# A longer modelled way from a transfer's end to its use, and two rings at the arena's other end

## The chip, the cores and the metric

The kernel runs on one core of a Trainium2 chip. The metric is the device time of one execution in microseconds (us). Engines are named as in the profile: PE is TensorE (PEld its weight loads), DVE is VectorE, ACT is ScalarE, POOL is GpSimd, SP is SyncE. POOL and SP compute next to nothing here: their queues issue the transfers.

## The reference, cut to what matters

A two-layer encoder trunk on 272 tokens of width 2048, in float32. Each layer is a mixer (an attention half and a state-space half, side by side) and a channel mixer (dense in layer 0, the best 2 of 8 experts in layer 1).

```python
for layer in range(2):
    hn = rms_norm(h, mix_norm[layer])
    c_q, c_kv, k_rope, u = jnp.split(hn @ w_in[layer], splits, axis=-1)
    att = mla_attention(c_q, c_kv, k_rope, ...)          # 8 heads
    ssm = s5_mixer(u, ...)                               # 64 groups of 16 channels, state 64, both directions
    mixed = jnp.concatenate([rms_norm(att, ...), rms_norm(ssm, ...)], -1)
    h = h + mixed @ w_out[layer]
    hn = rms_norm(h, ffn_norm[layer])
    h = h + (swiglu(hn, ...) if layer == 0 else moe_swiglu(hn, ...))
out = rms_norm(h, final_norm)[:, 16:]
```

`s5_mixer` is a linear recurrence over the tokens. It is computed here in chunks of 4 tokens: an input product per group (X), a scan over 68 chunks, and an output product per group (y).

## The kernel before

All weights (some 550 MB) stream from HBM once in blocks of 512 KB through a class `Stream` (five `raw` buffers; a high and a low part, `wh` and `wl`, are made of each block by ACT and DVE, and three products stand for one of float32). The first 40 blocks, of layer 0's mixer, are used as plain float32 (`raw` itself is the operand); one such product shows as two records in the trace.

**What sets the order.** The program is one stream of instructions, and every engine works its own part of it off strictly in order. Which instruction is written next is decided while the program is built: `Sched.run` holds a main generator (`mixer`, `dense`, `experts`) and a list of side generators. A generator yields a condition or a time; it goes on when the planner's clock, `Model.t["PE"]`, has come to it. `Model` keeps for each 16 bytes (or so) of memory the time at which it was last written and last read; `Model.run` moves an engine's time on by a planned cost, and `Model.dma` plans a transfer: issue 0.5 us (0.6 us on POOL's queue), 0.65 us, then the elements of the target at 90 per ns; `mark("DMA", ...)` then enters the end plus `OUT["DMA"]` as the time from which the target can be used (and the source written over). `Kern.rdy(...)` is that time plus 0.2 us, and a side generator that uses loaded data yields it ahead of its instructions. So `OUT["DMA"]` says how late after a transfer its users are written into the program. The hardware waits with semaphores in any case; only the order is planned.

**The chain around the change, in each mixer.** The main generator computes eight tiles of `u` (`u_tile`, 16 products of 128 x 272 each, in the order 0, 4, 1, 5, 2, 6, 3, 7). Each tile is scaled by DVE and put into the DRAM scratch `uscr` through POOL's queue (`put_u`). When the tiles `qb` and `qb + 4` are there, `ssm_x` loads them back in another layout (`load_u`, two transfers of 136 KB on POOL's queue), and its input products (`128x136` on PE, two for each group, between the products of `u`) read them. In layer 0 the matrices V of these products are made by DVE at that time (`v_make`, two `128x512` products of `ssm_bT` and `pscr` loads), as are the output matrices W and the Toeplitz blocks (`w_all`, `toep`: four products of `64x96` on PE; loads of `ssm_bz` and `ssm_C`). In layer 1 V and W were made ahead during `dense`. Then come the scan on DVE (`ssm_scan`), attention on PE (`attention`), and, once attention is over, the copies of the state (`ssm_h`, ring `rh`) and the output products (`ssm_y`, `68x64` on PE, ring `ry`), between the products of the first half of `w_out`. The gate's products (`w_glu`) behind it need all of `ssm_y`.

**Memory.** `Arena.get` hands out stretches of one large tile, first fit from the low end or, with `top=True`, from the high end; `room` asks whether requests fit, always from the low end.

Of the kernel before, what the change touches and what calls it, by code (L numbers as in the profile page):

```python
# [24 lines left out]
NC = 68  # L25
TC = 4
# [43 lines left out]
class Arena:  # L70


    def __init__(self, t, n):
        self.t, self.n, self.live = t, n, []
        self.peak = 0
# [52 lines left out]


class Ring:  # L130
    def __init__(self, arena, n, shape, p=128):
        self.h = [arena.get(shape, p) for _ in range(n)]
        self.i = 0

    def next(self):
# [109 lines left out]
class Model:  # L245


    OUT = {"PE": 197.0, "DVE": 127.0, "ACT": 152.0, "DMA": 960.0}

    def __init__(self):  # L250
        self.t = {"PE": 0.0, "DVE": 0.0, "ACT": 0.0, "DGE": 0.0, "DMA": 0.0}
# [84 lines left out]
    def mark(self, eng, e, ins, outs):  # L336
        e += self.OUT[eng]
        for ap in ins:
            n, u = self.where(ap)
            if u is not None:  # L340
                r = self.mem[n][1]
                r[u] = np.maximum(r[u], e)
        for ap in outs:
            n, u = self.where(ap)
            if u is not None:
                self.mem[n][0][u] = e

    def dma(self, q, out, *ins):
        t = max(self.q.get(q, 0.0), self.ready(*ins))
        n, u = self.where(out)  # L350
        if u is not None:
            t = max(t, self.mem[n][0][u].max(), self.mem[n][1][u].max())
        t = max(t, self.t["DGE"]) if q != "pool" else t
        e = t + (500.0 if q != "pool" else 600.0)
        self.q[q] = e
        if q != "pool":
            self.t["DGE"] = e
        d = max(self.t["DMA"], e + 650.0) + size_all(out) / 90.0
        self.t["DMA"] = d
        self.mark("DMA", d, ins, [out])  # L360
        if self.log is not None:
            self.log.append(("DMA", d - size_all(out) / 90.0, d, "dma"))
        return d + 960.0


def size_all(ap):
    n = 1
    for x in ap.shape:
        n *= x
    return n  # L370
# [161 lines left out]
class Kern:  # L532
# [568 lines left out]
    def ssm_h(self, l, F):  # L1101

        nc, st = self.nc, self.st
        yield self.has("scan", l)
        yield self.has("att", l)
        yield lambda: F.room(2 * 4 * 2 * NC)
        X = st["X"]
        rh = st["rh"] = Ring(F, 2, [4, 2, NC])
        st["hq"], st["hn"], n = [], 0, 0
        for t in rh.h:  # L1110
            nc.vector.memset(t.ap, 0.0)
        for T in TORD:
            for a in (0, 4):
                yield lambda: n - st["hn"] < 2
                t = rh.next()
                yield self.s.m.clear(t)
                g = 8 * T + a
                nc.scalar.activation(t[0:64, :, :, 1:NC],
                                     X[0:64, :, :, g:g + 4].rearrange("p s r g -> p g r s"), AF.Copy)
                nc.vector.tensor_copy(t[64:128, :, :, 0:NC - 1],  # L1120
                                      X[64:128, ::-1, :, g:g + 4].rearrange("p s r g -> p g r s"))
                st["hq"].append((t, self.rdy(t)))
                n += 1
# [153 lines left out]
    def ssm_y(self, l, F):  # L1277

        nc, st = self.nc, self.st
        q0 = NMETA if l else 0  # L1280
        N, k0 = L - q0, q0 // TC
        yield self.has("scan", l)
        yield lambda: "rh" in st and self.R is not None and F.room(8 * N, 512, 512) and self.R.room(8 * N, 8 * N)
        R = self.R
        g_ = st["g"] = F.get([8, N], top=True)
        gh, gl = st["gh"], st["gl"] = R.get([8, N]), R.get([8, N])
        ry = Ring(F, 2, [TC, 8, 16], NC)
        idn = self.cst[:NC, CI:CI + NC]

        def turn(T, y, t):  # L1290
            yield t
            bank = yield from self.grab()
            ps = bank[:, :L].rearrange("p (t k) -> p t k", t=TC)
            for j in range(TC):
                nc.tensor.transpose(ps[:, j], y[:, j].rearrange("p g c -> p (g c)"), idn)
            nc.scalar.activation(g_[:, T].rearrange("p (k t) -> p t k", t=TC), ps[:, :, k0:], AF.Gelu_apprx_tanh)
            self.drop(bank)
            nc.scalar.activation(gh[:, T], g_[:, T], AF.Copy)
            yield self.rdy(gh[:, T])
            nc.vector.tensor_tensor(gl[:, T], g_[:, T], gh[:, T].bitcast(F32), op=OP.subtract)  # L1300
            st["nT"] += 1

        st["nT"] = 0
        for i, T in enumerate(TORD):
            yield lambda: i in st["wq"]
            w, m, u, t = st["wq"].pop(i)
            yield t
            yield lambda: i - st["nT"] < 2
            y = ry.next()
            bank = yield from self.grab()  # L1310
            ps = bank[:NC].rearrange("p (g t c) -> p g t c", g=8, t=TC)
            for a in (0, 4):
                yield lambda: len(st["hq"]) > 0
                H, t = st["hq"].pop(0)
                yield t
                for g in range(4):
                    b = (a + g) // GW[l], (a + g) % GW[l]
                    for r in range(2):
                        nc.tensor.matmul(ps[:, a + g], H[:, g, r], w[:, b[0], r, :, b[1]], start=(r == 0), stop=False)
                    nc.tensor.matmul(ps[:, a + g], u[:, a + g, T // 4],  # L1320
                                     m[:, a + g].rearrange("p (t c) -> p t c", t=TC), start=False, stop=True)
                    if g % 2:
                        yield None
                st["hn"] += 1
            st["yn"] = i + 1
            nc.scalar.activation(y.rearrange("p t g c -> p g t c"), ps, AF.Copy)
            self.drop(bank)
            self.s.add(turn(T, y, self.rdy(y)))
        yield lambda: st["nT"] == 8
        for r in (ry, st["rh"], st["U"], st["X"]) + st["rw"]:  # L1330
            r.free()
        self.flags.add(("Y", l))
# [1058 lines left out]
```

## Time and profile before

| | us |
|---|---|
| device time, median of 3 runs | 2499.2 (2496.71 to 2500.32) |
| profiled execution | 2494.38 |
| its span, first to last instruction | 2492.5 |
| PE busy | 2427.1 (97%) |
| DVE busy | 1920.4 (77%) |
| ACT busy | 1375.0 (55%) |

In time, layer 0's input products begin at 47 us and layer 1's at 1311.60 us; all compute instructions carry line 408, that of the helper through which they are written, so groups are told apart by their tiles (`fa` is the float32 arena, `bank` a bank of PSUM). Ends of matmuls are modelled, so PE's waits are read from the idle time that stands in brackets ahead of a row, and its speed from the starts of rows that follow each other.

### The profile page before, as it was taken

The numbers are of one execution on the slowest core, as the hardware profiler recorded it, in microseconds if no ns is written. First come the engines' busy times: TensorE is split into PE (matmuls) and PEld (weight loads), VectorE is DVE, ScalarE is ACT, GpSimd is POOL, SyncE is SP. The second block draws the span as 40 slices with busy tenths as digits, with TensorE's granted clock in tenths as the row PEclk, the third lists the DMA queues.
The fourth block names the chain that finished last, engine by engine and source line by source line (L and its number), as shares of the span: only waits on it lengthen the run. The fifth ranks groups of instructions, "written<-read, shape, count | busy, mean of one in ns | idle before, by whom it ended". The sixth has DMA issues, their size and how long they took to land. (4 is left out here: it accounts for less than half of the span.)

```text
span 2492.5 us, 42294 instructions
## 1 busy us (share of the span) xinstructions
PE 2427.1 (97%) x15930; PEld 2187.0 (88%) x15930; DVE 1920.4 (77%) x3282; ACT 1375.0 (55%) x1876; POOL 152.2 (6%) x262
## 2 busy tenths in 40 slices
PE   8899999999999999999999899999999999999997
PEld 6676699999999999999999759987888888888886
DVE  8788657787766666555666987668999999999997
ACT  4324566443333333334455456546777877877775
POOL 3400110011100000000011001000000000000000
PEclk9999899999999999999999989999999999999998
DMA  7842554568755555555566316657999999999995
GB/s 258 230 149 86 141 157 151 167 215 269 261 187 194 188 191 190 172 177 170 178 205 195 127 44 204 236 201 271 387 355 350 385 341 371 365 330 372 360 336 198
DMA packets 192919, 583.47 MB, mean 234 GB/s; under 512 B 36225, under 2 KB 48897, under 8 KB 191553
## 3 DMA queue, kind: packets, MB, share of 16 engines
q1 hardware_dynamic: 174802, 520.42, 60.0%
q0 software_dynamic: 17040, 57.97, 7.7%
q8 instruction: 127, 2.08, 0.3%
q10 hardware_dynamic: 864, 2.28, 0.3%
q14 instruction: 86, 0.70, 0.1%
HBM read 560.14 MB, written 22.54 MB: 234 GB/s over the span
## 5 line engine op out<-in xcount | busy, mean ns | idle before, releaser
L408 DVE TENSOR_TENSOR wl<-raw,wh 128x1024 fp32r<-128x1024 f32 (+1 forms) x559 | 667.6, 1202 | 194.2 <-ACT wh L408 188.4
L408 ACT ACTIVATE wh<-raw 128x1024 fp32r<-128x1024 f32 (+1 forms) x559 | 579.8, 1040 | 318.9 <-PE bank L408 231.4
L408 PE MATMUL bank<-XH,wh 128*128 128x272 f32 (+1 forms) x2160 | 636.8, 295 | 0.8 <-ACT tmpr L408 0.5
L408 PE MATMUL bank<-XH,wl 128*128 128x272 f32 (+1 forms) x2160 | 623.0, 288 | 3.1 <-DVE wl L408 3.1
L408 PE MATMUL bank<-XL,wh 128*128 128x272 f32 (+1 forms) x2160 | 620.8, 287 | 1.6 <-DVE XL L408 1.3
L408 PEld LDWEIGHTS bank<-XH,wh 128*128 128x128 f32 x2160 | 407.6, 189 | 5.1 <-ACT tmpr L408 0.7
L408 PEld LDWEIGHTS bank<-XH,wl 128*128 128x128 f32 x2160 | 407.1, 188 | 4.5 <-DVE wl L408 4.5
L408 PEld LDWEIGHTS bank<-XL,wh 128*128 128x128 f32 x2160 | 407.9, 189 | 2.6 <-DVE XL L408 2.2
L408 PE MATMUL bank<-ra,wh 128*128 128x272 f32 (+1 forms) x1792 | 341.1, 290 | 1.8 <-ACT wh L408 1.8
L408 PEld LDWEIGHTS bank<-ra,wh 128*128 128x128 f32 x1792 | 280.7, 188 | 6.5 <-issue 2.4
L408 PE MATMUL bank<-fa 128*68 128x64 f32 (+11 forms) x1892 | 263.5, 279 | 21.9 <-DMA fa<-uscr 10.2
L408 PEld LDWEIGHTS bank<-fa 128*68 128x68 f32 (+6 forms) x1892 | 196.1, 161 | 83.8 <-issue 50.4
L408 DVE TENSOR_TENSOR fa<-fa 128x128 f32<-128x128 f32 (+9 forms) x687 | 236.2, 353 | 43.0 <-ACT fa L408 16.9
L408 PE MATMUL bank<-ra,wl 128*128 128x272 f32 (+1 forms) x896 | 256.6, 286 | 0.8 <-DVE wl L408 0.8
L408 PE MATMUL bank<-wh,XH 128*128 128x512 f32 (+1 forms) x584 | 222.6, 381 | 0.7 <-ACT fa L408 0.4
L408 ACT ACTIVATE fa<-bank 64x268 f32<-64x268 f32 (+9 forms) x281 | 138.6, 500 | 150.4 <-PE bank L408 133.2
L408 PE MATMUL bank<-wh,XL 128*128 128x512 f32 (+1 forms) x584 | 220.1, 377 | 0.0
L408 PE MATMUL bank<-wl,XH 128*128 128x512 f32 (+1 forms) x584 | 219.0, 375 | 0.0
L408 PE MATMUL bank<-wh,ra 128*128 128x512 f32 x552 | 185.7, 393 | 2.0 <-ACT fa L408 2.0
L408 PE MATMUL bank<-fa,raw 128*128 128x272 f32 x608 | 162.4, 405 | 7.2 <-DMA raw<-w_mix 6.4
L408 PEld LDWEIGHTS bank<-ra,wl 128*128 128x128 f32 x896 | 168.6, 188 | 1.0 <-DVE wl L408 1.0
L408 DVE TENSOR_TENSOR wl<-h,wh 128x1024 fp32r<-128x1024 f32 (+1 forms) x137 | 157.0, 1156 | 9.9 <-ACT wh L408 7.4
(127 smaller groups left out, 3232.6 us busy)
## 6 DMA issues: line engine op xcount, KB each, us to landing
raw<-w_dense SPq DMA_DIRECT2D x264, 512.0 KB, 3.4
raw<-w_mix SPq DMA_DIRECT2D x150, 512.0 KB, 3.4
raw<-w_moe_g SPq DMA_DIRECT2D x106, 512.0 KB, 5.5
h<-w_moe_g SPq DMA_DIRECT2D x80, 512.0 KB, 5.8
raw<-w_moe_d SPq DMA_DIRECT2D x73, 512.0 KB, 6.7
h<-w_moe_d SPq DMA_DIRECT2D x59, 512.0 KB, 6.6
raw<-w_moe_t SPq DMA_DIRECT2D x51, 384.0 KB, 4.0
h<-w_moe_t SPq DMA_DIRECT2D x44, 384.0 KB, 4.1
```

Source lines behind the costliest of these rows:

```text
L408: return f(*a, **k)
```

## The change

The planner's figure for the way from a transfer's end to its use is 2260 ns in place of 960 ns, in both places where it stands (the value that `dma` returns is used by nobody). `Ring` gets a `top` argument, and the rings `rh` and `ry` are taken from the high end of their arena. No instruction is added or removed: each engine has the same instructions, of the same shapes, in another order.

```diff
 class Ring:
-    def __init__(self, arena, n, shape, p=128):
-        self.h = [arena.get(shape, p) for _ in range(n)]
+    def __init__(self, arena, n, shape, p=128, top=False):
+        self.h = [arena.get(shape, p, **({"top": True} if top else {})) for _ in range(n)]
...
-    OUT = {"PE": 197.0, "DVE": 127.0, "ACT": 152.0, "DMA": 960.0}
+    OUT = {"PE": 197.0, "DVE": 127.0, "ACT": 152.0, "DMA": 2260.0}
...
-        return d + 960.0
+        return d + 2260.0
...
-        rh = st["rh"] = Ring(F, 2, [4, 2, NC])
+        rh = st["rh"] = Ring(F, 2, [4, 2, NC], top=True)
...
-        ry = Ring(F, 2, [TC, 8, 16], NC)
+        ry = Ring(F, 2, [TC, 8, 16], NC, top=True)
```

On PE the order differs in the first 1,100 of its rows (layer 0's mixer up to the output products) and again in layer 1's mixer (its input products and its output products); `dense`, layer 1's attention and the experts' first pass keep theirs, word for word. On DVE and ACT single instructions move in the same stretches and in `dense`.

PE, layer 0, the second pair of `u` tiles. Its last product stands one row ahead of the first row here (bank_65); from there to the first input product that reads it (the last row) PE has before:

```order
L408 MATMUL bank_66<-fa,raw_99 128x272 x3
L408 MATMUL bank_71<-fa 128x136 x2
L408 MATMUL bank_66<-fa,raw_99 128x272
L408 MATMUL bank_68<-fa 128x136 x2
L408 MATMUL bank_66<-fa,raw_99 128x272 x4
L408 MATMUL bank_66<-fa,raw_100 128x272 x3
L408 MATMUL bank_69<-fa 64x96 x4
L408 MATMUL bank_66<-fa,raw_100 128x272 x3
L408 MATMUL bank_70<-fa 64x96 x4
L408 MATMUL bank_66<-fa,raw_100 128x272 x2
L408 MATMUL bank_71<-fa 128x136 x2
```

and now, where two products, one pair of input products and one Toeplitz block stand between the tile's last product and the first row here:

```order
L408 MATMUL bank_71<-fa 128x136 x2
L408 MATMUL bank_66<-fa,raw_99 128x272 x5
L408 MATMUL bank_68<-fa 128x136 x2
L408 MATMUL bank_66<-fa,raw_99 128x272
L408 MATMUL bank_69<-fa 128x136 x2
L408 MATMUL bank_66<-fa,raw_100 128x272 x2
L408 MATMUL bank_70<-fa 64x96 x4
L408 MATMUL bank_66<-fa,raw_100 128x272 x6
L408 MATMUL bank_67<-fa,raw_96 128x272 x3
L408 MATMUL bank_71<-fa 64x96 x4
L408 MATMUL bank_67<-fa,raw_96 128x272
L408 MATMUL bank_68<-fa 128x136 x2
```

The input product that reads the pair stood behind 16 products, 2 pairs and 2 Toeplitz blocks; it stands behind 20, 4 and 3.

PE, layer 0, the fourth and last pair. The tile's last product stands just ahead of the first row (in bank_66), the first input product that reads the pair is the last row. Before:

```order
L408 MATMUL bank_71<-fa 64x96 x4
L408 MATMUL bank_67<-fa,raw_97 128x272 x8
L408 MATMUL bank_67<-fa,raw_98 128x272
L408 MATMUL bank_68<-fa 64x96 x4
L408 MATMUL bank_67<-fa,raw_98 128x272 x3
L408 MATMUL bank_69<-fa 64x96 x4
L408 MATMUL bank_67<-fa,raw_98 128x272 x3
L408 MATMUL bank_70<-fa 128x136 x2
```

and now:

```order
L408 MATMUL bank_68<-fa 128x136 x2
L408 MATMUL bank_69<-fa 128x136 x2
L408 MATMUL bank_67<-fa,raw_97 128x272 x3
L408 MATMUL bank_70<-fa 64x96 x4
L408 MATMUL bank_67<-fa,raw_97 128x272 x5
L408 MATMUL bank_67<-fa,raw_98 128x272 x3
L408 MATMUL bank_71<-fa 64x96 x4
L408 MATMUL bank_67<-fa,raw_98 128x272 x3
L408 MATMUL bank_68<-fa 64x96 x4
L408 MATMUL bank_67<-fa,raw_98 128x272 x2
L408 MATMUL bank_65<-fa,raw_99 128x272 x2
L408 MATMUL bank_69<-fa 128x136 x2
```

It stood behind 15 products and 3 Toeplitz blocks; it stands behind 18 products, 2 pairs (of the third pair of tiles, moved back likewise) and 3 blocks.

PE, layer 1, the first pair of `u` tiles (here each product is three rows). Before, the first input product of the layer (the row with `128x136`) stands in the middle of the tile that follows the next one, 63 matmuls behind the pair's last:

```order
L408 MATMUL bank_67<-XH,wh_103 128x272
L408 MATMUL bank_67<-XL,wh_103 128x272
L408 MATMUL bank_67<-XH,wl_106 128x272
L408 MATMUL bank_69<-fa 128x136 x2
L408 MATMUL bank_67<-XH,wh_103 128x272
L408 MATMUL bank_67<-XL,wh_103 128x272
L408 MATMUL bank_67<-XH,wl_106 128x272
L408 MATMUL bank_68<-fa 128x136 x2
```

and now it stands behind that tile's end, 96 matmuls behind the pair's last, and three pairs follow each other at once:

```order
L408 MATMUL bank_67<-XL,wh_101 128x272
L408 MATMUL bank_67<-XH,wl_104 128x272
L408 MATMUL bank_68<-fa 128x136 x2
L408 MATMUL bank_69<-fa 128x136 x2
L408 MATMUL bank_71<-fa 128x136 x2
L408 MATMUL bank_65<-XH,wh_102 128x272
L408 MATMUL bank_65<-XL,wh_102 128x272
L408 MATMUL bank_65<-XH,wl_105 128x272
L408 MATMUL bank_70<-fa 128x136 x2
```

In the same way the first pair of layer 0 goes from 25 products and 1 block to 28 and 2, its third from 19 and 3 blocks to 20, 3 blocks and a pair, and layer 1's second, third and fourth pair from 63 matmuls each to 80, 96 and 80.

## Rows read from the trace of the kernel before

**Rows 1.** The page: busy time of each engine with its share of the span, and the clock granted to PE in 40 equal slices (tenths of full speed).
```profile
PE 2427.1 (97%) x15930; PEld 2187.0 (88%) x15930; DVE 1920.4 (77%) x3282; ACT 1375.0 (55%) x1876; POOL 152.2 (6%) x262
...
PEclk9999899999999999999999989999999999999998
```

**Rows 2.** The waits of PE over the whole span, longest in total first: us in total, times, the longest.
```profile
PE bank L408 <- DMA fa<-uscr: 10.2, 5, 3.0
PE bank L408 <- DVE XL L408: 8.4, 7, 1.9
PE bank L408 <- DMA raw<-w_mix: 6.4, 1, 6.4
...
PE bank L408 <- DMA fa<-xtok,fa: 4.5, 2, 3.0
```

**Rows 3.** PE in order of time around the second pair of layer 0: start, us from there to the end of the last in the row, records; in brackets the idle time ahead and what ended it.
```profile
57.88 3.37 PE L408 MATMUL bank<-fa,raw 128*128 128x272 f32 x14
61.18 0.88 PE L408 MATMUL bank<-fa 128*64 128x96 f32 x8
61.98 1.64 PE L408 MATMUL bank<-fa,raw 128*128 128x272 f32 x6
...
68.44 0.92 PE L408 MATMUL bank<-fa 128*128 128x136 f32 x4 [2.71 <-DMA fa<-uscr]
```

**Rows 4.** POOL's queue at the same place: the second tile's store, then the two loads.
```profile
58.87 0.56 POOL L390 DMA_DIRECT2D uscr<-fa  x1
59.42 0.71 POOL L390 DMA_DIRECT2D fa<-uscr  x1
64.63 0.70 POOL L390 DMA_DIRECT2D fa<-uscr  x1 [4.50 <-DMA uscr<-fa]
```

**Rows 5.** PE and POOL at the other places where PE waited for these loads: the first pair of layer 0, the first and the third of layer 1.
```profile
47.05 1.18 PE L408 MATMUL bank<-fa 128*128 128x136 f32 x8 [1.25 <-DMA fa<-uscr]
...
1304.48 0.55 POOL L390 DMA_DIRECT2D uscr<-fa  x1 [7.49 <-issue]
...
1311.60 1.25 PE L408 MATMUL bank<-fa 128*128 128x136 f32 x4 [2.57 <-DMA fa<-uscr]
...
1345.48 0.70 PE L408 MATMUL bank<-fa 128*128 128x136 f32 x4 [0.58 <-DMA fa<-uscr]
```

**Rows 6.** PE at the fourth pair of layer 0, and behind it.
```profile
125.73 0.70 PE L408 MATMUL bank<-fa 128*128 128x136 f32 x4 [3.04 <-DMA fa<-uscr]
126.27 0.62 PE L408 MATMUL bank<-fa,raw 128*128 128x272 f32 x2
126.72 1.02 PE L408 MATMUL bank<-fa 128*128 128x136 f32 x4
127.54 1.11 PE L408 MATMUL bank<-fa,raw 128*128 128x272 f32 x2
128.44 1.11 PE L408 MATMUL bank<-fa 128*128 128x136 f32 x4
129.35 1.06 PE L408 MATMUL bank<-fa,raw 128*128 128x272 f32 x2
130.25 0.94 PE L408 MATMUL bank<-fa 128*128 128x136 f32 x6
```

**Rows 7.** PE at the third pair of layer 0, which did not wait.
```profile
100.43 0.63 PE L408 MATMUL bank<-fa 128*128 128x136 f32 x4
100.89 0.62 PE L408 MATMUL bank<-fa,raw 128*128 128x272 f32 x2
...
102.28 0.40 PE L408 MATMUL bank<-fa 128*128 128x136 f32 x2
```

**Rows 8.** Stretches of the span: from, to, length; busy us of PE, PEld, DVE, ACT and POOL with their records; then PE's granted clock (1.00 is full), the DMA engines' busy share and GB/s.
```profile
68.78:72.19 3.41, 3.41 (x18) 2.94 (x17) 2.19 (x7) 1.69 (x4) 0.00 (x0) 0.50 0.45 112
...
126.80:130.21 3.41, 3.41 (x13) 3.00 (x12) 1.80 (x6) 3.04 (x6) 0.55 (x1) 0.50 0.64 197
1311.23:1314.64 3.41, 3.04 (x13) 3.08 (x14) 0.61 (x1) 0.80 (x2) 0.00 (x0) 0.50 0.32 130
276.99:290.64 13.65, 13.65 (x48) 8.12 (x47) 6.76 (x27) 5.17 (x15) 3.04 (x5) 0.50 0.54 119
1478.48:1495.55 17.07, 16.13 (x37) 8.45 (x37) 13.24 (x55) 5.29 (x15) 0.49 (x1) 0.50 0.00 1
92.67:96.08 3.41, 3.41 (x12) 2.61 (x11) 2.49 (x11) 0.33 (x1) 1.27 (x2) 0.50 0.81 185
...
800.00:850.00 50.00, 50.00 (x401) 48.94 (x400) 33.26 (x52) 17.84 (x20) 1.61 (x3) 1.00 0.60 196
...
1360.00:1480.00 120.00, 108.65 (x683) 89.28 (x682) 107.71 (x326) 65.41 (x140) 0.00 (x0) 0.98 0.31 101
```

**Rows 9.** The instructions on the tile `uscr` in the first 350 us, 8 stores and 16 loads: time from issue to landing.
```profile
DMA to landing us min/median/max: 2.1/5.0/6.2
```

**Rows 10.** DVE at a V product of layer 0, and PE at the Toeplitz block that reads what DVE makes behind it.
```profile
87.42 1.61 DVE L408 TENSOR_TENSOR fa<-fa 128x512 f32<-128x512 f32 x3 [4.01 <-DMA fa<-ssm_bT]
...
91.59 0.35 PE L408 MATMUL bank<-fa 128*64 128x96 f32 x2 [2.17 <-issue]
```

**Rows 11.** PE in order of time at a wait of attention in layer 0 and at one in layer 1.
```profile
275.58 0.41 PE L408 MATMUL bank<-cst,fa 96*16 96x96 f32 x3 [1.21 <-DVE XL L408]
...
1479.05 3.23 PE L408 MATMUL bank<-fa 128*128 128x272 f32 x5 [1.90 <-DVE XL L408]
```

## The prediction, made before the changed kernel ran

> **What bounds the kernel now.** I read the page first: PE is busy for 97% of the span, no other engine for more than 77% [rows 1]. So the time is PE's work plus the moments in which PE stands still or runs slowly, and a change of order alone can only move those. The reader should see how small they are: the listed waits of PE are a few us each, and the largest group, 10.2 us in five waits, is for the loads of `uscr` [rows 2]. The wait for `w_mix` is the start of the kernel and stays.
>
> Next I read PE's timeline at those waits. In layer 0, PE stands 2.71 us ahead of the second pair's first input product [rows 3]; POOL's queue shows why: the store of the second tile is issued at 58.87, the second load can go only when it has landed, at 64.63, and the product starts at 68.44, 9.6 us after the store's issue [rows 4]. The fourth pair waits 3.04 us [rows 6], the first 1.25 us, layer 1's first pair 2.57 us and its third 0.58 us [rows 5]. The third pair of layer 0, whose loads came in time, runs on without a gap [rows 7].
>
> Then the clock. After the waits of 2.71, 3.04 and 2.57 us the granted clock is 0.50 for 3.41 us, the lower of the two levels, 1.2 GHz [rows 8]. Its price is read from equal work: two pairs of input products and two products of `u` take 126.72 to 130.25 = 3.53 us there [rows 6] and 100.43 to 102.28 = 1.85 us at full clock [rows 7]; so 1.7 us each time. No such stretch follows the 1.25 and 0.58 us waits.
>
> **The change part by part.** *The planner's figure.* It adds no instruction. It plans the users of loaded data 1.3 us later, and those behind a store and a load 2.6 us later. By its rules a load of `uscr` took 0.60 + 0.65 + 0.39 + 0.96 = 2.6 us and takes 3.9 now; the trace has 5.0 in the middle of its stores and loads, 2.1 to 6.2 [rows 9]. So the users were written in too early for this chain, and are so still, by less.
>
> What counts on PE is the work that stands between the tile's last product and the first input product. A product of `u` takes (61.18 - 57.88) / 7 = 0.47 us (two records each), a Toeplitz block 61.98 - 61.18 = 0.80 us [rows 3], a pair of input products 100.89 - 100.43 = 0.46 us [rows 7]. With the counts of the order:
> - second pair: 16 x 0.47 + 2 x 0.46 + 2 x 0.80 = 10.0 us before, 20 x 0.47 + 4 x 0.46 + 3 x 0.80 = 13.6 now. 3.6 more covers the wait of 2.71: gain 2.71.
> - fourth pair: 9.45 before, 18 x 0.47 + 2 x 0.46 + 3 x 0.80 = 11.8 now. 2.3 of 3.04 are covered: gain 2.3, and 0.7 stay.
> - first pair: 25 products and 1 block, 12.6, become 28 and 2, 14.8. It gains its 1.25. The third gets 0.9 more and needs none.
> - layer 1: 401 matmuls in 50 us [rows 8] are 0.125 us each; the first and third pair get 33 more, 4.1 us. Gain 2.57 + 0.58. The second and fourth get 2.1 that they don't need.
>
> The waits give 9.4 us, and the three slow-clock stretches that followed them 3 x 1.7 = 5.1 us, if they go as well. Sum 14.5 us.
>
> *What moves along.* V products and Toeplitz blocks move in layer 0. One place there already costs: DVE stands 4.01 us for a load of `ssm_bT`, and 4 us later PE stands 2.17 us at the Toeplitz block that waits for DVE's queue [rows 10], with a slow-clock stretch behind it [rows 8]. Between that V product and that block the order has the same PE work before and now (5 products and a block), so I count it neither gone nor worse. Other blocks come closer to what they read: the 17th stands 0.2 us of PE work behind the last DVE operation on its W, where 2.3 us stood. What this costs is not shown; it is bounded by nothing below (the order leaves it enough if DVE is not late) and by one more such wait, 2.17 + 1.7 = 3.9 us, above. I take half, 2.0.
>
> The stores that SP's queue issues (`wscr`, `escr`) stand elsewhere among the weight loads. PE waited for a weight block in the mixers only at the start [rows 2], and five blocks are under way; so nothing, at worst one wait like the 0.58 us one. The input products end 3 products (1.4 us) later in layer 0's order and 9 matmuls (1.1 us) later in layer 1's, so the scan starts that much later relative to PE. Attention's products cover it. The output products move back by 12 matmuls in layer 0 and 12 to 15 in layer 1. They lie among `w_out`'s first half: their last transpose leaves 210 matmuls, 26 us, ahead of `w_glu` in layer 0 and 60, 7.5 us, in layer 1. So nothing; without this cover, up to 1.9 us.
>
> *The rings at the other end* cost no instruction. What they may add is a wait of the ring's first writer for the last reader of what lay there; the stores of `w_all`, which holds the high end, have been waited for when it is freed. I take nothing, at most one DVE wait of the longest kind here, 4.01 us [rows 10], which PE would see only through the 26 us above.
>
> The experts start in the same order; their `xtok` waits of 4.5 us [rows 2] stay.
>
> Sum: 14.5 - 2.0 = 12.5 us. On the profiled execution, 2494.4 us (its span is 1.9 us less), that makes 2481.9. The median of the three runs is 4.8 us above that execution, and the forecast is made against it: 2499.2 - 12.5 = 2486.7 us.
>
> **The rivals.**
> *The waits move and do not go (no change).* What PE truly lacks may be DVE, which is busy for 107.71 of 120 us in layer 1's attention [rows 8]. PE then reaches attention up to 9 us earlier and gives it back at DVE's queue. For it: the waits for `XL`, 8.4 us in seven [rows 2], are there already, and their order stays. Against it: three of the five waits are in layer 0, and the brackets name the loads. If layer 1's 3.15 + 1.7 and half of layer 0's 9.7 come back, 4.8 - 2.0 = 2.8 us are left: 2496.
>
> *The old figure was right (no change).* If a transfer of this chain landed within the 2.6 us that the planner gave it before, the moved products would only start later, with nothing saved and, by the cover above, nothing lost: 2499. The fastest row is 2.1 us, but the middle is 5.0 [rows 9], and three of the chains end in a wait whose bracket names the load [rows 3, 5, 6]; so 0.04. The Trainium skill, DMA: Bandwidth & Descriptors, section Anatomy of one DMA — SWDGE (gpsimd) path, speaks for this rival: a fixed 2.0 us for a transfer plus its bytes at 436 GB/s, for 136 KB an estimate of 2.3 us by that page. The trace disagrees with it by its 5.0 us.
>
> *Slower: the clock in attention of layer 0.* A wait of only 1.21 us at 275.58 [rows 11] stood ahead of 13.65 us at the lower clock [rows 8]. Attention there is small plain float32 products, and the Toeplitz blocks between its heads move. Each us more at the lower clock costs 0.5 us of PE time; the gain is used up when 25 us more of it fall to 0.50 than now. If 52 us more of it do (four stretches like that one in place of one would be 41 us more), that is 26 - 12.5 = 13 us: 2513. Against it: only that one stretch is slow now, and the order moves blocks by one head at most.
>
> *Faster than forecast.* The same lottery the other way: the stretches of 13.65 and 17.07 us [rows 8], behind waits of 1.21 and 1.90 us [rows 11], cost up to 6.8 and 8.5 us. Layer 1's attention keeps its order, so I give only the first a chance to go: 2480; both: 2471.
>
> **How the numbers follow.** Forecast, 2482 to 2493: 0.50. Faster than that: 0.14. No change, 2494 to 2504: 0.20 for the waits that move and 0.04 for the old figure, 0.24. Slower: 0.12. Within 0.2% (5.0 us) a measurement of this kernel can't tell a change from none; so faster 0.64, same 0.24, slower 0.12. The range reaches from the better case's 2477 to 2503, and leaves out the far ends of the lottery, some 0.17. The forecast's own range is 2482 to 2493: its upper end is the waits alone without the clock and with 3.9 us of new waits (9.4 - 3.9 = 5.5), its lower end all of 14.5 and the block's 2.17.
>
> **What would show it.** In the profile of the changed kernel PE's waits for `fa<-uscr` should be under 2 us in total instead of 10.2, the only one left that of layer 0's fourth pair, about 0.7 us; the granted clock should be 1.00 in the stretches behind the four pairs; PE's wait at the tenth Toeplitz block should still be there. The forecast is wrong if those waits go and the time does not (then look at DVE's waits and at the clock in attention), or if they stay because the store and load land later than 9 us after the store's issue.

## The result, and the profile after

The changed kernel takes 2476.55 us (median of 6 runs, 2475.24 to 2481.03), the kernel before 2496.45 us in the 6 runs beside it (2493.45 to 2500.32). The ratio is 0.9921 with an interval of [0.9908, 0.9934]: 16.5 to 23 us faster, 19.7 in the middle. The forecast was 12.5 us and 2486.7; the time lies 0.45 us below the lower end of the range, 2477.0. The direction and the place were right, the size was too small.

The profiled execution after takes 2478.65 us, its span is 2476.9 us. The page, busy time of each engine and the clock granted to PE in 40 slices, answers to [rows 1]:

```profile
PE 2417.3 (98%) x15930; PEld 2181.0 (88%) x15930; DVE 1920.8 (78%) x3282; ACT 1375.1 (56%) x1876; POOL 151.5 (6%) x262
...
PEclk9999999999999999999999989999999999999998
```

Read it against the span. PE's idle time went from 2492.5 - 2427.1 = 65.4 us to 2476.9 - 2417.3 = 59.6 us, which is 5.8 us; its busy time fell by 9.8 us with the same 15930 instructions. Most of this pair's 15.6 us are therefore not waits but instructions that no longer run at half clock: by the clock records the granted clock is 0.50 for 64.9 us of the trace before and 41.0 us of the trace after, the stretch at the very end left out, and half of the 23.9 us between is 12, a part of which falls into idle time.

The waits of PE over the whole span (us in total, times, the longest) answer to [rows 2]:

```profile
PE bank L408 <- DVE XL L408: 9.3, 8, 1.9
PE bank L408 <- DMA raw<-w_mix: 6.5, 1, 6.5
PE bank L408 <- ACT fa L408: 6.1, 6, 2.0
PE bank L408 <- issue: 4.8, 6, 2.0
PE bank L408 <- DMA fa<-xtok,fa: 4.4, 2, 3.2
...
PE bank L408 <- DMA fa<-uscr: 1.0, 2, 0.7
```

The loads of `uscr` have gone from 10.2 us in five waits to 1.0 in two. But a group's name is what the profile could attribute; PE in order of time at the four pairs of layer 0 and the first of layer 1 (start, us, records, idle time ahead in brackets) shows what is left:

```profile
48.00 0.63 PE L408 MATMUL bank<-fa 128*128 128x136 f32 x4
...
68.41 0.70 PE L408 MATMUL bank<-fa 128*128 128x136 f32 x4 [1.53 <-issue]
...
99.60 0.79 PE L408 MATMUL bank<-fa 128*128 128x136 f32 x4 [2.05 <-issue]
...
101.20 5.00 PE L408 MATMUL bank<-fa,raw 128*128 128x272 f32 x14
...
118.66 0.70 PE L408 MATMUL bank<-fa 128*128 128x136 f32 x4 [0.27 <-DMA fa<-uscr]
...
1311.93 0.70 PE L408 MATMUL bank<-fa 128*128 128x136 f32 x4 [0.72 <-DMA fa<-uscr]
```

The first pair runs on ([rows 5] had 1.25 ahead of it), the fourth keeps 0.27 of 3.04 [rows 6], layer 1's first 0.72 of 2.57. At the second pair 1.53 of 2.71 us remain, and the profile names nothing for them. POOL's queue there answers to [rows 4]:

```profile
57.40 0.55 POOL L390 DMA_DIRECT2D uscr<-fa  x1 [0.31 <-DVE fa L408]
...
62.89 0.69 POOL L390 DMA_DIRECT2D fa<-uscr  x1 [1.20 <-DMA uscr<-fa]
```

The second load is issued 5.5 us ahead of the product; the tile's own view gives 2.4, 5.3 and 8.7 us from issue to landing (shortest, middle, longest) for these transfers, so that this load landed just then is likely and not shown. The wait of 2.05 us at 99.60 is new. Ahead of it DVE waits for a store of W; DVE in order of time:

```profile
94.01 0.63 DVE L408 TENSOR_TENSOR fa<-Wp,fa 128x192 f32<-128x192 f32 x2 [3.31 <-DMA wscr<-fa]
...
102.76 2.28 DVE L408 TENSOR_TENSOR fa<-fa 128x512 f32<-128x512 f32 x4 [1.74 <-DMA fa<-ssm_bT]
```

What is missing from this queue matters more. DVE's waits in the first 200 us of the kernel before, and of the kernel after, by what ended them (us in total, times, the longest):

```profile
DVE fa L408 <- DMA fa<-ssm_bT: 12.4, 5, 4.0
...
DVE fa L408 <- DMA wscr<-fa: 3.6, 3, 1.9
```

```profile
DVE fa L408 <- DMA wscr<-fa: 4.4, 2, 3.3
DVE fa L408 <- DMA fa<-ssm_bT: 2.9, 2, 1.7
```

DVE waited 12.4 us for the loads of `ssm_bT`, from which the matrices V are made, and waits 2.9 now: the longer figure moves the V products away from their loads too. The wait of 4.01 us among them, and the Toeplitz block that stood behind it [rows 10], are gone.

Stretches of the span after (from, to, length; busy us of PE, PEld, DVE, ACT, POOL with records; granted clock, DMA share, GB/s): behind the second pair, behind the wait at 99.60, and attention of layer 0, where [rows 8] has 13.65 us at 0.50.

```profile
68.41:71.82 3.41, 3.41 (x23) 3.04 (x23) 3.31 (x9) 2.60 (x5) 2.62 (x6) 1.00 1.00 316
101.07:104.48 3.41, 3.41 (x11) 2.60 (x10) 1.58 (x3) 1.86 (x3) 0.63 (x2) 0.50 1.01 292
262.00:290.00 28.00, 26.25 (x167) 18.53 (x166) 21.10 (x70) 17.70 (x41) 7.57 (x13) 1.00 0.49 141
```

### The profile page after: what moved, and what is told of

It reads as the page before. It is cut to its first block, busy times and chain, and to the rows that moved or that the text cites. A ratio compares the mean times of both kernels' runs of the same rounds, so it can differ in the third digit from the quotient of the medians.

```text
span 2476.9 us, 42278 instructions
## 1 busy us (share of the span) xinstructions
PE 2417.3 (98%) x15930; PEld 2181.0 (88%) x15930; DVE 1920.8 (78%) x3282; ACT 1375.1 (56%) x1876; POOL 151.5 (6%) x262
## 5 line engine op out<-in xcount | busy, mean ns | idle before, releaser
L408 PE MATMUL bank<-fa 128*68 128x64 f32 (+10 forms) x1892 | 252.9, 272 | 16.5 <-DVE XL L408 5.0
L408 DVE TENSOR_TENSOR fa<-fa 128x128 f32<-128x128 f32 (+9 forms) x687 | 236.6, 353 | 32.6 <-ACT fa L408 15.6
L408 PEld LDWEIGHTS bank<-fa 128*68 128x68 f32 (+5 forms) x1892 | 188.9, 156 | 75.3 <-issue 42.1
```

The costliest lines, as they stand in the source:

```text
L408: return f(*a, **k)
```

## The experiments

The kernels with one part of the change were built from the changed kernel with the figure back at 960 ns, so that their rings lie at the high end. Ratios are against the kernel before in the same series. Edits are quoted in the shortest form that says them.

### Which part

**The rings alone.**

```diff
-    OUT = {"PE": 197.0, "DVE": 127.0, "ACT": 152.0, "DMA": 2260.0}
+    OUT = {"PE": 197.0, "DVE": 127.0, "ACT": 152.0, "DMA": 960.0}
```

> The two rings alone at the arena's high end, the planner's figure at 960 ns. Every engine then has the order of the kernel before, so only addresses differ. Theory (all of the gain is the order): no change, within 3 us of before, the waits for fa<-uscr 10 us in total as before. Rival (the rings' place removes waits for the last readers of the low end): faster by 5 us or more.

Measured 2494.06 against 2497.24, ratio 0.9991 [0.9973, 1.0009]. The theory held: every engine's order is the same as before, and no change is clear of noise. PE's waits for `fa<-uscr` are 14.8 us, not 10; the old order's own executions below reach as far. The opposite part, the longer figure with the rings at the low end, does not exist as a kernel: with it the planner finds no room for the copies of the state or the output products in layer 0. The rings are what lets the longer figure be planned.

**The longer figure in one layer's mixer.** `late` is 1300 in layer 0's mixer and 0 elsewhere, then the other way round.

```diff
-        self.mark("DMA", d, ins, [out])
+        self.mark("DMA", d + self.late, ins, [out])
```

> The longer figure in layer 0's mixer alone (rings high throughout). Theory (layer 0 makes the whole gain, layer 1's is given back at DVE in its attention): 15 to 19 us faster, as much as the whole change within 2 us. Rival (the sum on record, where layer 1 keeps 4.9 us and layer 0's net is 7.7): about 8 us faster, and 5 us or more short of the whole change.

Measured 2487.33, ratio 0.9960 [0.9945, 0.9975]: 10 us, 6 to 14 by the interval. The theory of 15 to 19 fell; the sum on record, 8, lies inside.

> The longer figure in layer 1's mixer alone. Theory (given back at DVE): 0 to 2 us faster; the two waits for fa<-uscr there, 3.15 us, nearly gone, and new waits for wl and wh of about 3 us some 50 us later. Rival (the sum on record): 4.9 us faster.

Measured 2489.21, ratio 0.9976 [0.9959, 0.9993]: 6 us, 1.7 to 10 by the interval. The theory that layer 1's saving is given back at DVE, which I had formed after the result, allowed it 0 to 2 us. The interval alone just touches that; the trace decides against it: layer 1's input products take 56.9 us there, 61.6 to 65.1 in the old order, and its attention 139.7, within the old order's 138.0 to 140.3.

**Layer 0's input products alone.** The longer figure ends with the last input product of layer 0.

```diff
-        self.flags.add(("X", l))
+        self.flags.add(("X", l)); self.s.m.late = 0.0
```

> The longer figure only until the last input product of layer 0 is written; attention, the output products and all that follows are planned with 960 ns. Theory: the order around the input products makes 9 us, and the Toeplitz blocks that it moves into other places of attention decide the clock there, another 4 to 6 us: 13 to 15 us faster, and no stretch of 13.65 us at the lower clock in attention. Rival (planning the rest with the longer figure makes the second part): 9 to 10 us faster.

Measured 2485.44, ratio 0.9959 [0.9942, 0.9976]: 10 us, as much as the longer figure in the whole of layer 0's mixer. The rival's 9 to 10 us lie in the middle of the interval, 6 to 14.5, the theory's 13 to 15 at its end, and its sign failed: a wait of 1.21 us stayed in attention, and the profiled execution has 27.3 us at half clock behind it.

**The whole again.** The changed kernel as it is.

> The changed kernel once more, beside the runs below. Theory (the gain is the waits for the uscr loads and the clock stretches behind them, 14.5 us, and what lies above is scatter of the clock elsewhere): 13 to 17 us faster. Rival (a further gain that the sum on record lacks): 18 to 22 us faster again.

Measured 2478.87, ratio 0.9924 [0.9907, 0.9942]: 19 us. The middle fits the rival, but the interval, 14.5 to 23 us, reaches into the theory's 13 to 17, and the profiled executions below give 16.7: whether the first result was a favourable draw stays open. The layers' 10 and 6 add up to 16; the rest is within the intervals.

### Which transfers

**`uscr` alone, and all but `uscr`.** The edit of the first; the second has the two figures exchanged.

```diff
-        self.mark("DMA", d, ins, [out])
+        self.mark("DMA", d + (1300.0 if any("uscr" in a.tensor.name for a in (out, *ins)) else 0.0), ins, [out])
```

> The longer figure for the transfers to and from uscr alone, 960 ns for all others. Theory (this chain makes the gain): 12 to 16 us faster, PE's waits for fa<-uscr under 3 us in total. Rival (the loads for V, W and the Toeplitz blocks, planned later too, make a good part): 6 to 10 us faster.

Measured 2483.04, ratio 0.9943 [0.9923, 0.9964]: 14 us, 9 to 19 by the interval; the theory held.

> The longer figure for all transfers but those to and from uscr. Theory (the uscr chain makes the gain): within 3 us of before, and PE still waits 8 us or more for fa<-uscr. Rival (the other loads make a good part): 5 to 9 us faster, DVE's wait of 4 us for ssm_bT gone.

Measured 2500.22, ratio 1.0004 [0.9988, 1.0021]: nothing, as the theory had it. PE's waits over the span, first of the `uscr` kernel, then of the other:

```profile
PE bank L408 <- DVE fa L408: 7.4, 6, 3.6
...
PE bank L408 <- DMA fa<-uscr: 2.6, 2, 1.8
```

```profile
PE bank L408 <- DMA fa<-uscr: 15.1, 6, 6.0
```

So the chain through `uscr` is needed, and without it the rest is worth nothing: what DVE gains then does not reach PE, whose idle time in layer 0's input products is 14.6 us, against 10.1 to 14.4 in five executions of the old order. But the rest is not idle either. In the `uscr` kernel PE still waits for DVE in layer 0, and DVE for `ssm_bT`; PE's row, then DVE's, and DVE's waits for that load in the first 200 us of this kernel and of the other, where DVE waits for ACT instead (3.9 to 5.7 us in the old order):

```profile
83.19 2.71 PE L408 MATMUL bank<-fa 128*128 128x136 f32 x12 [3.56 <-DVE fa L408]
```

```profile
81.14 2.49 DVE L408 TENSOR_TENSOR fa<-fa 128x512 f32<-128x512 f32 x5 [3.43 <-DMA fa<-ssm_bT]
```

```profile
DVE fa L408 <- DMA fa<-ssm_bT: 7.2, 4, 3.4
```

```profile
DVE fa L408 <- ACT fa L408: 17.3, 10, 4.2
...
DVE fa L408 <- DMA fa<-ssm_bT: 1.3, 2, 0.7
```

DVE's waits for `ssm_bT` in the first 200 us are 11.0 to 14.2 us in seven profiled executions of layer 0's old order, 7.2 in this kernel, 1.3 with all but `uscr`, and 2.2 to 2.9 in four executions of the whole change. The 5 us between this kernel and the whole fit that, though their intervals overlap.

### What could take some of it back

**The scan of layer 1 left out**, with the old figure and with the new.

```diff
-        for s in range(1, NC - 1):
+        for s in range(1, 0 if l else NC - 1):
```

> The scan of layer 1's state-space half left out (66 steps of four DVE operations), planner's figure at 960 ns, rings high. Both theories: faster than before by what DVE's scan costs PE in layer 1's attention. It is the base for the next run.

> The changed kernel with the same scan left out. Theory (in layer 1, DVE's scan takes back about 2 us of the 4.7 us that the input products gain): layer 1, from its first products to the end of its attention, is 4 to 5 us shorter here than in the run before, against 2.8 us with the scan in; in all 16 to 22 us faster than the run before. Rival (what attention loses has nothing to do with the scan, as its clock): no more than 3 us shorter there.

Measured 2498.53, ratio 0.9998 [0.9983, 1.0014], and 2479.64, ratio 0.9921 [0.9903, 0.9938]. Without the scan the change is worth the same by the medians. Layer 1 from its first products to the end of its attention is 4.2 us shorter with the new figure, as the theory said (185.4 and 181.2 us); but with the scan in, the means of the executions below give 5.8 us there, not the 2.8 of a single pair. So no run shows that the scan's DVE work costs PE anything or eats the saving.

**More of it.** The figure at 3560 ns; and the changed kernel with the stores of `wscr` counted 1500 ns later still, against the wait at 99.60.

```diff
-    OUT = {"PE": 197.0, "DVE": 127.0, "ACT": 152.0, "DMA": 2260.0}
+    OUT = {"PE": 197.0, "DVE": 127.0, "ACT": 152.0, "DMA": 3560.0}
```

> The figure at 3560 ns, twice the step. Theory (a wait can only be removed once): nothing more to gain from uscr's loads, so 10 to 16 us faster than before, no faster than the whole change. Rival (the more the later): 4 us or more faster than the whole change. If the longer chain runs out of cover, slower than the whole change by 5 us or more, with new waits of PE in layer 0's input products.

Measured 2484.30, ratio 0.9944 [0.9924, 0.9963]: 14 us, no better than the change; the intervals overlap. The theory held. PE's waits for ACT are 11.9 us in fourteen there, 6.1 in six after the change; seven of them, 0.7 to 1.0 us each, stand among layer 1's output products, from 1537 to 1564 us, so what falls short there is not layer 0's input products.

```profile
PE bank L408 <- ACT fa L408: 11.9, 14, 1.8
...
PE bank L408 <- DMA fa<-uscr: 2.7, 2, 2.0
```

```diff
-        self.mark("DMA", d, ins, [out])
+        self.mark("DMA", d + (1500.0 if "wscr" in out.tensor.name else 0.0), ins, [out])
```

> The changed kernel, and the stores to wscr counted 1.5 us later still. In the changed kernel DVE waits 3.3 us for such a store at 94 us and PE 2.05 us behind it, with a slow-clock stretch. Theory (the same mechanism one transfer further): that wait goes, 2 to 4 us faster than the changed kernel. Rival (the wait moves to the Toeplitz blocks, which then stand closer to DVE): no faster than it, within 2 us.

Measured 2484.97, ratio 0.9953 [0.9933, 0.9973]: 12 us faster than before, 7 less than the change, with intervals that overlap. It is not faster, so the theory fell. The wait at 99.60 went, one of 2.60 us at the second pair came:

```profile
68.93 0.70 PE L408 MATMUL bank<-fa 128*128 128x136 f32 x4 [2.60 <-DMA fa<-uscr]
```

No version was found that beats the changed kernel.

### How much one execution tells

**Further profiled executions of both kernels**, one each.

> The kernel before, one more profiled execution, to see how much its waits for uscr vary: theory (the waits in its profile are one draw of several): its first 325 products take 135 to 143 us (137.2 in the profile shown), their waits 6 to 17 us.

> The kernel before, another profiled execution. Theory (the old order's length scatters because its waits are set by when transfers land, and single clock stretches fall into attention): layer 0's first 325 products 135 to 143 us; layer 1's first 360 products 60 to 66 us; now and then 5 to 10 us more in an attention. Rival (something outside these stretches differs): dense or the experts differ by 2 us or more between the orders.

> The changed kernel, another profiled execution. Theory: 125 to 128 us, 57 to 58 us at the same places, no clock stretch in layer 0's attention. Rival (something outside these stretches differs): dense or the experts are shorter than in the old order by 2 us or more.

> As the first run of this set, a third draw of the same kernel: 135 to 143 us and 60 to 66 us at the two places by the theory; by the rival the difference lies in dense or the experts.

> As the second run of this set: 125 to 128 us and 57 to 58 us at the two places by the theory; by the rival the difference lies in dense or the experts.

They took 2494.35, 2494.81 and 2501.73 us (before), 2475.96 and 2480.90 us (after). Two lengths fall just outside what was expected for layer 0's input products, 134.3 us (old order, 135 to 143) and 129.5 (new, 125 to 128); the others fit, and the rest of the kernel is not shorter in the new order, against the rival. With the runs above that makes five profiled executions in the old order (the rings alone have it word for word) and four in the new. PE's products with a weight block as operand come in the same sequence in both, so the starts of the same products cut every execution into the same pieces of work; "half clock" is the time in a piece at which the granted clock was 0.50, from each trace's clock records. Means, in us, with the single executions in brackets:

| piece | old order | new order | gain |
|---|---|---|---|
| layer 0, input products | 137.4 (134.3 to 141.8) | 127.1 (125.2 to 129.5) | 10.3 |
| of it at half clock | 7.5 (3.4 to 10.2) | 1.7 (0 to 3.4) | |
| layer 0, attention | 202.7 (199.4 to 207.5) | 199.8 (199.7 to 199.8) | 2.9 |
| of it at half clock | 7.5 (13.7, 0, 3.4, 20.5, 0) | 0 (0, 0, 0, 0) | |
| layer 1, input products | 62.9 (61.6 to 65.1) | 57.5 (57.4 to 57.6) | 5.4 |
| of it at half clock | 3.4 (0 to 6.8) | 0 | |
| all the rest | 2090.9 | 2092.8 | -1.9 |
| sum | 2493.9 | 2477.2 | 16.7 |

In attention, all five old executions and the two others profiled with the same attention order (layer 1 alone, and the old figure without the scan) have one wait of 1.21 or 1.22 us near 275 us, as [rows 11] has it; all four new ones, layer 0 alone and the new figure without the scan have two of 0.59 to 0.61. PE in order of time in the kernel after:

```profile
265.90 0.40 PE L408 MATMUL bank<-cst,fa 96*16 96x96 f32 x3 [0.60 <-DVE XL L408]
...
274.68 0.40 PE L408 MATMUL bank<-cst,fa 96*16 96x96 f32 x3 [0.59 <-DVE XL L408]
```

Of those seven, three have half clock right behind the one wait, for 13.7, 20.5 and 20.5 us; the 3.4 us in the table come 15.6 us later, behind a wait for ACT. Of the six, none has. Four kernels with other orders in attention also have one wait of 1.21 us: layer 0's input products alone with 27.3 us at half clock behind it, `uscr` alone, all but `uscr` and 3560 ns with none. (The kernel with `wscr` later has two waits of this length and 3.4 us at half clock.) That is 4 in 11 against 0 in 6, and with a chance of 4 in 11 each, six executions would have none about once in 15.

The same cut shows what the parts do in layer 0, from the first to the 1,401st record of a product with a weight block, where all these orders have done the same work on PE: 420.8 us in the old order, 407.9 in the new (means), 415.6 with `uscr` alone, 422.2 with all but `uscr`. With `uscr` alone PE's idle time in the input products is 10.0 us, hardly below the old order's mean of 11.7; in the new order it is 3.6 to 5.7. So together the parts gain 12.9 us there, alone 5.2 and -1.4, as far as one execution of each can tell.

## Why the forecast had the sign and missed the size

**The waits for `uscr`: right, but not enough alone.** Without the chain nothing is gained, and the figure does it, not the rings (`uscr` alone 14 us, all others nothing, rings nothing). The step "PE's waits for `fa<-uscr` should be under 2 us in total" held: 1.0 (1.2 to 1.5 in the three other executions). By name only: the unnamed 1.53 us at the second pair is probably the same chain (layer 0 alone, with the same order there, has 1.43 us at that product and names the load; the three other executions of the change have 0.2 to 0.4), and that pair's 2.71 was counted as wholly covered.

**The clock behind these waits: right in size.** I took three stretches, 5.1 us. The means fall by 7.5 - 1.7 + 3.4 = 9.2 us at half clock in the two layers' input products, worth 4.6 us at half speed. Of the old order's 7.5, 1.4 stood behind the Toeplitz block's wait and not behind these; the new order's 1.7 stand behind its new wait. One reading was loose: layer 1's stretch, from 1311.23, begins 0.37 us before its wait ends at 1311.60, and not after it.

**The step that failed: "What this costs is not shown; ... I take half, 2.0."** I charged 2.0 us for blocks that come closer to what they read, and of the V product and the tenth block I wrote "I count it neither gone nor worse". I had looked at the work between that V product and the block, and not at the work between the load of `ssm_bT` and the V product, which the same figure lengthens. DVE's waits for that load fell from 12.4 to 2.9 us, and the block's 2.17 us (0.2 to 2.17 in the old order's five executions), which "should still be there", went. In its place came 1.2 to 2.1 us at an input product, with half clock behind it in two of four executions. Input products of both layers gave 10.3 + 5.4 = 15.7 us; less the clock's 4.6 that is 11.1 of waits, where I had 9.4 - 1.1 = 8.3 (the other 0.9 of the 2.0 stood for the clock). Layer 0 carries this error: 10.3 against 2.71 + 2.3 + 1.25 + 3.4 - 2.0 = 7.7. Layer 1's 5.4 stands against 2.57 + 0.58 + 1.7 = 4.85.

**The clock in attention of layer 0** was put into a rival at 0.14 and added nothing to the sum. It gave 2.9 us on the mean, and 4.8 (204.6 - 199.8) against the one execution that I had. That the split of the one wait into two is the cause is suggested by 4 in 11 executions against 0 in 6, and not shown: no kernel changed that wait alone, and none in six may be luck. The timed runs point both ways. Layer 0 alone has the split and layer 0's input products alone has not, and both gain 10 us; but the first's six runs lie within 8 us and the second's twelve within 17.

**The rivals.** "The waits move and do not go" fell with layer 1 alone (6 us) and with the scan left out (same gain). It is true of the parts: with all but `uscr` PE's `uscr` waits stay, 15.1 us against 7.5 to 14.8, and with `uscr` alone PE waits for DVE instead. "The old figure was right" fell with `uscr` alone. The Trainium skill, DMA: Bandwidth & Descriptors, section Anatomy of one DMA — SWDGE (gpsimd) path, would have kept it with its estimate of 2.3 us. The trace disagrees: 5.3 us were measured in the middle after the change. The slower one, clock in attention, went the other way. The output products' cover and the rings at nothing are borne out within the scatter: the rest of the kernel got 1.9 us longer, about what its pieces differ between executions of one order.

**What stays open.** The gain is 10.3 + 2.9 + 5.4 - 1.9 = 16.7 us by the profiled executions and 19 to 20 by the medians of timed runs. The 3 us between lie inside the ratio's interval, 16.5 to 23; timed runs leave no trace, so nothing places them. Of the 10.1 us between 2486.7 and 2476.55, 2.75 come from the median before, 2499.2 in three runs and 2496.45 in six. The time missed the range by 0.45 us, less than that, so to fall outside was in part the draw of three runs; the gain, 19.7 for 12.5, was too small by either.

## What to carry to other kernels

A planner's latency figure touches every transfer that it plans: before one mover of waits is costed, list the other engines' waits for transfers (here DVE's 12.4 us for `ssm_bT`) and ask of each whether it goes too, since here the waits removed on one queue alone were in good part waited for on the next. Set the figure by the measured way through the longest chain and try beyond it: 2260 ns gave 19 us here, 3560 ns 14, with intervals that overlap. And profile the kernel before several times, because PE's waits for `uscr` ranged from 7.5 to 14.8 us in five executions of one order.

## What the runs showed of the hardware that was not expected

The same order of instructions with the same wait ahead ran at half clock in one execution and at full clock in another. Two further executions of the kernel before, each with PE at the wait in order of time and then the stretch behind it as above; first the one of 2501.73 us:

```profile
276.75 0.41 PE L408 MATMUL bank<-cst,fa 96*16 96x96 f32 x3 [1.21 <-DVE XL L408]
```

```profile
277.00:298.00 21.00, 21.00 (x72) 12.39 (x70) 9.22 (x38) 7.33 (x21) 5.76 (x10) 0.54 0.46 104
```

and the one of 2494.35 us:

```profile
275.49 0.40 PE L408 MATMUL bank<-cst,fa 96*16 96x96 f32 x3 [1.21 <-DVE XL L408]
```

```profile
276.00:297.00 21.00, 19.25 (x113) 13.15 (x112) 12.98 (x42) 12.10 (x27) 6.51 (x10) 1.00 0.59 148
```

In 21 us PE got through 72 records at a mean of 0.54 and 113 at 1.00. The scatter is smaller after the change: profiled attention of layer 0 spread over 8.1 us in the old order and 0.1 us in the new, and the changed kernel's 12 timed runs lie within 5.8 us, against 16.2 for 21 runs of the kernel before. That the waits removed are what took it along is likely and not shown.
